# The opening of a two-layer hybrid trunk: another order of loads, plain products for half of the inner dimension, and a bank of its own for the first compression

## The chip, the cores and the metric

One core of one Trainium2 chip runs the whole program. The metric is the device time of one execution in microseconds. The kernel before took 2611.32 us (median of three runs, from 2610.13 to 2612.88).

## The reference

Two layers work on `x` of 1024 positions by 1024 features, with a condition `c` of 1024 numbers. Cut to what this case needs:

```python
cond = jax.nn.silu(c)
for l in range(2):
    mod = cond @ w_mod[l] + b_mod[l]                       # 6 x 1024
    sh1, sc1, gt1, sh2, sc2, gt2 = split(mod, 6)
    h = rms_norm(x, norm_g[l, 0]) * (1.0 + sc1) + sh1
    p = h @ w_in[l]                                        # 22 blocks of 128 columns
    outs = [conv(p), sparse_attention(p), linear_attention(p), gmlp(p)]
    y = rms_norm(outs, grp_gain[l]) @ w_o[l]
    x = x + gt1 * rms_norm(y, norm_g[l, 1])
    h = rms_norm(x, norm_g[l, 2]) * (1.0 + sc2) + sh2
    y = jnp.square(jax.nn.relu(h @ w_up[l])) @ w_down[l]
    x = x + gt2 * rms_norm(y, norm_g[l, 3])
```

The sparse attention compresses its keys and values first: windows of 32 positions of `k_cmp` and `v_cmp`, with the rows of `cmp_pos` added, go through `silu(z @ cmp_w1) @ cmp_w2`. Queries and keys of its other two branches (selected and sliding window) are rotated by cosine and sine of `positions`.

## The kernel before, in words

Activations lie with features on partitions: a tile is 128 features by T = 512 positions, and `x` is two halves of eight such tiles. A product of the projections is made in three products of a rounded type (`mm3`, L174 to L177): each operand is split into a rounded `hi` (a cast on ACT) and the rest `lo` (a subtraction on DVE), and TensorE adds `hi*hi`, `hi*lo` and `lo*hi`. Products of two plain fp32 operands are used where tiles are small, for the sums over partitions with a matrix of ones (L199) and for transposes.

`start()` (L269) is the opening of layer 0, first half:
- `rope_tables()` (L346 to L390) loads the frequencies, a selection matrix and the positions, makes cosine and sine in some 30 small DVE steps, spreads them with TensorE through a bank of tag `s`, and stores four tables to DRAM (L390).
- `cond` is loaded in two halves, spread over all partitions, and takes `silu` (L293 to L296).
- `load_x` loads eight tiles; `rms_R` (L190 to L199) squares them on ACT, adds the squares on DVE, and makes one product with `ones`; `rstd` (L202) gives R by two activations, `Ln` and `Exp`.
- for each of eight k: two rows of `w_mod` (shift and scale) are loaded (128 x 1024, L276) and each is multiplied by `cond` and summed on DVE (`mod_dot`, L239 to L243); `make_h` (L207 to L215) makes `h` of k as `hi` and `lo`; six column blocks of `w_in` (`EARLY`, 10 and 17 to 21) take their products of this k, each in a PSUM bank of its own (two of `mm`, two of `ff`, two of `s`). The weights of these blocks come in two halves of four k (`wload`, L279), and are split at k = 0 and k = 4 (`wsplit`, L284).
- `load_params` (L107) loads the small vectors of both layers on SP's queue.

Everything behind it is in `mix(0, 0, ...)`. There are lanes of streamed weights, each with its own buffers: `a` (always there), `b` (region "wb", opened at L925 for the first `mix` alone) and `f` (for the feed-forward part). A region takes its memory where an earlier region was closed; a tile in it waits for the last use of what lay there. `start()` has regions "kw" (right side), "su" and "rp". In the first `mix` the remaining sixteen column blocks go through `gemm` (L179) in lane `b`: two halves of four k, each one load (L158), one split (L167 and L131) and twelve products; beside each half, a step of `mods_now` (L322) loads and multiplies one more row of `w_mod` in two halves (`mod_half`, L245 to L251, loads into `raw_b`). The sparse attention (`nsa_part`) runs between them: `compress` (L702 to L756), then for each of four blocks of 128 positions scores (L829, L831), softmax, and `attend` (L780 to L790): four transposes of the weights into the one bank of tag `t`, a cast, a subtraction, two products into the bank of tag `pv`. I call one such group an attention unit. Each of the four mixers ends in a group norm (`group_out`, L218, with a product with `ones`), and then the eight gemms with `w_o` start (lane `a`).

PSUM has eight banks: two each of `mm`, `ff` and `s`, one of `t` and one of `pv` (L58). `compress` takes four tiles in turn from `mm`, the tag that the gemms use:

```python
            hx = partial(lambda jj, i: k5[:, jj, i // 8:i // 8 + 32, 2 * (i % 8)])
            hp_ = ps("mm", (128, 2, 32))
...
                hb = partial(lambda jj, i: pos2[:, jj, 2 * i:2 * i + 32])
                pb = ps("mm", (128, 2, 2))
```

`hx` is the pass over the keys and values (32 small products, L717), `hb` the same pass over the position rows, which are loaded at L732.

The order on each engine is not written by hand: the whole kernel stands in a block whose scheduler lists the instructions of each engine from a simulated time line, so an edit in one place moves instructions in others. One queue, SP's, issues all DMAs.

Of the kernel before, what the change touches and what calls it, by code (L numbers as in the profile page):

```python
# [35 lines left out]
def trunk_kernel(ctx, tc, xT, c, pos, freq, sel, w_in, conv_w, cmp_pos, cmp_w1, cmp_w2,  # L36
# [10 lines left out]
    def region(name, side="left"):  # L47
        return tc.tile_pool(name=name, bufs=1, reuse_waits="tile", side=side)
# [58 lines left out]
    def load_params(l, names):  # L107
        src = {"ng": norm_g, "bmod": b_mod, "conv": conv_w, "gain": gains}
        for n in names:
            dma(out=par[l][n], in_=src[n][l])  # L110
# [95 lines left out]

    def make_h(xt, R, Ac, shc, ks=range(8)):  # L207
        h = []
        for k in ks:
# [59 lines left out]
    def start():  # L269
        d = par[0]  # L270
        early = {}
        rope_tables()
        with region("kw", "right") as kw, region("su") as su:
            def mk(src, shape):
                t = su.tile(shape, F32, name="mw", tag="mw", bufs=4)
                dma(out=t, in_=src)  # L276
                return t

            def wload(n, kh):  # L279
                raw = kw.tile([128, 4, 128], F32, name="raw_k", tag="raw_k", bufs=6)  # L280
                dma(out=raw, in_=w_in[0, n, :, 4 * kh:4 * kh + 4, :])
                return raw

            def wsplit(raw):  # L284
                hi, lo = (kw.tile([128, 4, 128], F32R, name="w_k", tag="w_k", bufs=12) for _ in range(2))
                A.copy(hi, raw)
                sub(lo, raw, hi.bitcast(F32))
                return hi, lo

            for hf in range(2):  # L290
                t1, t2 = (su.tile([128, T], F32, name="ct", tag="ct", bufs=4) for _ in range(2))
                ch = cond[:, hf * T:hf * T + T]
                dma(out=ch, in_=c[:, hf * T:hf * T + T].to_broadcast([128, T]))  # L293
                logsig(t2, ch, t1)
                A.activation(t2, t2, AF.Exp)
                mul(ch, ch, t2)  # L296
            xt = load_x(0)
            load_params(0, ("ng", "bmod"))
            R = rms_R(xt, 1.0 / 1024)
            bm = d["bmod"].rearrange("p (j k) -> p j k", k=8)  # L300
            hs = []
            for k in range(8):
                ma = work.tile([128, 2, 1], F32, name="ma", tag="ma", bufs=4)
                for j in (0, 1):
                    mod_dot(0, j, k, mk, ma[:, j, :])
                add(d["mod"][:, 0:2, k:k + 1], ma, bm[:, 0:2, k:k + 1])
                mod_scale(0, 1, slice(k, k + 1))
                if k % 4 == 0:
                    raws = [wload(n, k // 4) for n in EARLY]
                hs += make_h(xt, R, d["A1"], d["mod"][:, 0, :], (k,))  # L310
                if k % 4 == 0:
                    ws = {n: wsplit(r) for n, r in zip(EARLY, raws)}
# [6 lines left out]
        load_params(1, ("ng", "bmod", "conv", "gain"))  # L319
        return hs, early  # L320

# [24 lines left out]
    def rope_tables():  # L346
        with region("rp") as rp:
# [3 lines left out]
            fr = rp.tile([128, 1, 8], F32, name="fr")  # L351
            dma(out=fr, in_=freq.unsqueeze(0).to_broadcast([128, 1, 8]))
            sl = rp.tile([17, 256], F32, name="sl")
            dma(out=sl, in_=sel)
            pi = rp.tile([128, 8, 1], I32, name="pi")
            dma(out=pi, in_=pos.unsqueeze(2))
# [22 lines left out]
            for hf in range(2):  # L379
# [5 lines left out]
                for w, dst in ((0, cosd), (128, sind)):  # L385
                    p = ps("s")
# [243 lines left out]
    def nsa_part(l, hf, h, rg, gates, early={}):  # L630
# [70 lines left out]

        def compress():  # L702
# [8 lines left out]
            def partial(col):  # L711

                hid = ps("mm", (128, 2, 128))
# [9 lines left out]
            hx = partial(lambda jj, i: k5[:, jj, i // 8:i // 8 + 32, 2 * (i % 8)])  # L723
            hp_ = ps("mm", (128, 2, 32))
            for jj in range(2):
                PE.matmul(hp_[:, jj, :], hx[:, jj, :], sel4, start=True, stop=True)
            if hf == 0:
# [7 lines left out]
                pb = ps("mm", (128, 2, 2))  # L735
                for jj in range(2):
                    PE.matmul(pb[:, jj, :], hb[:, jj, :], sel4[:, 0:2], start=True, stop=True)
                A.copy(posb[l], pb[:, :, 0:1])
            hs = pt((128, 2, 32))
# [5 lines left out]
            kc = ps("mm", (128, 2, 64))  # L745
# [6 lines left out]
            vc = ps("mm", (128, 64))  # L752
# [314 lines left out]

    h, early = start()
# [96 lines left out]
```

## Time and profile before

| | before |
|---|---|
| median of three runs | 2611.32 us |
| profiled execution | 2618.0 us |
| its span | 2616.3 us |
| PE (TensorE) busy | 2488.0 us, 95% |
| PEld (its weight loads, beside PE) | 1985.6 us, 76% |
| DVE (VectorE) busy | 1631.3 us, 62% |
| ACT (ScalarE) busy | 1308.9 us, 50% |
| POOL (GpSimd) busy | 53.9 us, 2% |
| DMA | 305.79 MB, mean 117 GB/s |
| chain that ended last | PE 83%, DVE 8%, DMA 5%, ACT 2%, issue 1% |

The profile shows one execution; its own time is 1.7 us above its span and 6.7 us above the median. Busy time is the time in which an engine worked on instructions; the chain is the work followed back from the last instruction, at each step to what released it. The granted clock is the share of TensorE's full clock that it had in a stretch. In the rows below a line number stands before each operation (L175), and "out<-in" are the program's names.

### The profile page before, as it was taken

The page shows a single profiled execution, that of the slowest core. Times are in us where ns is not written, and L with a number is a line of the kernel's source. Part 1 is how long each engine was busy: PE and PEld are TensorE (multiplying, and loading weights), DVE is VectorE, ACT ScalarE, POOL GpSimd, SP SyncE. Part 2 cuts the span into 40 slices and gives each one's busy share as a digit, 9 for nine tenths or more (in the row PEclk, how much of TensorE's full clock was granted, in tenths as well). Part 3 has the DMA queues.
Part 4 walks back from the last instruction along what each step waited for, and adds up shares of the span by engine and source line. Part 5 has one row for each costly group of instructions (what it writes and reads, how often), then busy time and mean ns, then how long its engine had stood idle before and what let it go on. Part 6 is the DMA issues. An engine that isn't in the chain of part 4 may idle for free.

```text
span 2616.3 us, 34392 instructions
## 1 busy us (share of the span) xinstructions
PE 2488.0 (95%) x11834; PEld 1985.6 (76%) x11834; DVE 1631.3 (62%) x3425; ACT 1308.9 (50%) x2657; POOL 53.9 (2%) x65
## 2 busy tenths in 40 slices
PE   5798899999999999999999999999999997999997
PEld 3666677777777878887787787877788875788886
DVE  7697675467887587445676476554577745634445
ACT  3465545445565456344365455444466744443433
POOL 0100000010000000000100000000100000000000
PEclk9898899999999999999999999999999999999999
DMA  8443233355434444223423354322422134333332
GB/s 280 141 151 94 91 122 121 110 152 153 127 117 142 153 157 146 93 78 105 146 77 92 94 157 141 103 81 77 121 74 69 61 107 150 127 98 97 97 97 75
DMA packets 176200, 305.79 MB, mean 117 GB/s; under 512 B 21573, under 2 KB 33434, under 8 KB 176026
## 3 DMA queue, kind: packets, MB, share of 16 engines
q1 hardware_dynamic: 176026, 303.60, 37.6%
q8 instruction: 93, 1.52, 0.2%
q14 instruction: 81, 0.66, 0.1%
HBM read 281.50 MB, written 17.83 MB: 114 GB/s over the span
## 4 chain that ended last, share of the span: by engine, by line
PE 83%; DVE 8%; DMA 5%; ACT 2%; issue 1%; SPq 0%; DVEq 0%; ACTq 0%
PE ps_ff L175 17%; PE ps_ff L176 17%; PE ps_ff L177 17%; PE ps_mm L176 7%; PE ps_mm L177 7%; PE ps_mm L175 7%; DMA raw_f<-in_w_mod_dram 2%; PE ps_mm L784 1%; DMA raw_b<-in_w_mod_dram 1%; PE ps_pv L790 1%; PE ps_pv L789 1%; PE ps_s L829 1%; PE ps_t L199 1%; PE ps_s L831 1%; PE ps_t L784 1%
## 5 line engine op out<-in xcount | busy, mean ns | idle before, releaser
L167 ACT CAST w_f<-raw_f 128x512 fp32r<-128x512 f32 x504 | 311.8, 619 | 430.5 <-PE ps_ff L176 409.0
L131 DVE TENSOR_TENSOR w_f<-raw_f,w_f 128x512 fp32r<-128x512 f32 x504 | 350.7, 697 | 177.7 <-ACT w_f L167 166.6
L175 PE MATMUL ps_ff<-hid,w_f 128*128 128x512 f32 x992 | 395.2, 399 | 21.4 <-DVE yf L137 12.7
L177 PE MATMUL ps_ff<-h,w_f 128*128 128x512 f32 x1024 | 405.4, 396 | 1.2 <-DVE w_f L131 1.2
L176 PE MATMUL ps_ff<-h,w_f 128*128 128x512 f32 x1024 | 402.7, 393 | 0.0
L175 PE MATMUL ps_ff<-h,w_f 128*128 128x512 f32 x1024 | 402.7, 393 | 0.0
L176 PE MATMUL ps_ff<-hid,w_f 128*128 128x512 f32 x992 | 392.1, 395 | 1.5 <-DVE hid L131 1.5
L177 PE MATMUL ps_ff<-hid,w_f 128*128 128x512 f32 x992 | 391.3, 394 | 0.0
L175 PE MATMUL ps_mm<-h,w_a 128*128 128x512 f32 x784 | 317.1, 405 | 6.2 <-ACT h L226 5.1
L177 PE MATMUL ps_mm<-h,w_a 128*128 128x512 f32 x784 | 315.7, 404 | 6.7 <-DVE w_a L131 6.7
L176 PE MATMUL ps_mm<-h,w_a 128*128 128x512 f32 x784 | 313.6, 401 | 1.2 <-DVE h L131 1.2
L167 ACT CAST w_a<-raw_a 128x512 fp32r<-128x512 f32 x196 | 121.3, 620 | 297.7 <-PE ps_mm L176 276.8
L131 DVE TENSOR_TENSOR w_a<-raw_a,w_a 128x512 fp32r<-128x512 f32 x196 | 135.0, 690 | 171.2 <-ACT w_a L167 167.3
L175 PEld LDWEIGHTS ps_ff<-hid,w_f 128*128 128x128 f32 x992 | 187.8, 189 | 69.7 <-DVE yf L137 15.2
L177 PEld LDWEIGHTS ps_ff<-h,w_f 128*128 128x128 f32 x1024 | 192.3, 188 | 45.8 <-issue 3.4
L175 PEld LDWEIGHTS ps_ff<-h,w_f 128*128 128x128 f32 x1024 | 192.4, 188 | 42.6 <-issue 3.1
L176 PEld LDWEIGHTS ps_ff<-h,w_f 128*128 128x128 f32 x1024 | 192.4, 188 | 42.0 <-issue 2.2
L176 PEld LDWEIGHTS ps_ff<-hid,w_f 128*128 128x128 f32 x992 | 187.9, 189 | 44.4 <-issue 2.9
L177 PEld LDWEIGHTS ps_ff<-hid,w_f 128*128 128x128 f32 x992 | 187.8, 189 | 41.2 <-issue 1.4
L137 DVE TENSOR_TENSOR y<-y,ps_ff 128x512 f32<-128x512 f32 (+1 forms) x208 | 138.0, 664 | 123.7 <-PE ps_ff L177 122.4
L175 PEld LDWEIGHTS ps_mm<-h,w_a 128*128 128x128 f32 x784 | 149.3, 190 | 45.8 <-ACT h L226 6.7
L177 PEld LDWEIGHTS ps_mm<-h,w_a 128*128 128x128 f32 x784 | 149.0, 190 | 44.9 <-DVE w_a L131 8.6
(390 smaller groups left out, 3618.3 us busy)
## 6 DMA issues: line engine op xcount, KB each, us to landing
raw_f<-in_w_up_dram SPq DMA_DIRECT2D x256, 256.0 KB, 2.7
raw_f<-in_w_down_dram SPq DMA_DIRECT2D x256, 256.0 KB, 2.7
raw_a<-in_w_in_dram SPq DMA_DIRECT2D x132, 256.0 KB, 2.7
raw_f<-in_w_mod_dram SPq DMA_DIRECT2D x112, 256.0 KB, 2.8
raw_a<-in_w_o_dram SPq DMA_DIRECT2D x64, 256.0 KB, 2.7
raw_b<-in_w_mod_dram SPq DMA_DIRECT2D x48, 256.0 KB, 2.9
mw<-in_w_mod_dram SPq DMA_DIRECT2D x16, 512.0 KB, 5.1
bp<-in_cmp_w_dram SPq DMA_DIRECT2D x32, 256.0 KB, 5.3
```

The costliest lines, as they stand in the source:

```text
L131: V.tensor_tensor(out=out, in0=a, in1=b, op=ALU.subtract)
L137: eng.tensor_tensor(out=out, in0=a, in1=b, op=ALU.add)
L167: A.copy(hi, raw)
L175: PE.matmul(ps_ap, wh, xh, start=start, stop=False)
L176: PE.matmul(ps_ap, wh, xl, start=False, stop=False)
L177: PE.matmul(ps_ap, wl, xh, start=False, stop=stop)
L199: PE.matmul(p, ones, acc, start=True, stop=True)
L784: PE.transpose(tp[0:kn, hh, :], cols(h0 + hh), ident)
L789: PE.matmul(pv[:, h0:h0 + nh, :], vst, th[0:kn], start=first[0], stop=False)
L790: PE.matmul(pv[:, h0:h0 + nh, :], vst, tl[0:kn], start=False, stop=last)
L829: PE.matmul(sp[:, 0:w], qh[:, h0 + hh, :], KX[:, 128 * k0:128 * k0 + w], start=True, stop=False)
L831: PE.matmul(sp[:, 0:w], ql[:, h0 + hh, :], KX[:, 128 * k0:128 * k0 + w], start=False, stop=True)
```

## The change

Five things are done.
1. `start()`: `cond` is loaded first (SP), then two rows of `w_mod`, then `x`, then the six `w_in` halves and the next four rows; the small vectors and the three inputs of the tables go to POOL's queue (`P.dma_start`). Two more buffers take rows of `w_mod` (6 instead of 4), and rows are loaded three k ahead. The second halves of the six blocks lie in buffers of tag `h`.
2. The squares of `x` are summed by TensorE: eight fp32 products with `ones`, one for each k, in place of seven additions on DVE and one product.
3. For the first four k the six blocks take one plain fp32 product each, of the raw weights and the unsplit `h`, in place of three products of split operands. `h` of each k is still split, since the later gemms use it. `x` is multiplied by R first, and one activation with scale and shift makes `h`. The six splits of the first halves go away; those of the second halves stand behind k = 1.
4. `rope_tables` comes last in the code of `start()`, and its products take the bank of `pv`.
5. Region "wb" is opened before `start()` (it no longer lies where the opening's buffers lay). In the first `mix` `compress` takes its four tiles from the bank of `pv`, and the pass over the position rows stands ahead of the pass over keys and values, in every `mix`.

```diff
+        with region("kw", "right") as kw, region("rp") as rp, region("su") as su:
...
+            for c_ in halves:
+                dma(out=cond[:, c_], in_=c[:, c_].to_broadcast([128, T]))
+            load_params(0, ("ng", "bmod"), P.dma_start)
+            small = rope_loads(rp)
+            mws = {0: mload(0)}
+            xt = load_x(0)
+            raws = [wload(n) for n in EARLY]
+            mws[1] = mload(1)
+            mws[2] = mload(2)
+            late = [wlate(n) for n in EARLY]
...
-            R = rms_R(xt, 1.0 / 1024)
+            p = ps("t")
+            for k in range(8):
+                sq = nt()
+                A.activation(sq, xt[k], AF.Square)
+                PE.matmul(p, ones, sq, start=k == 0, stop=k == 7)
+            R = rstd(p, 1.0 / 1024, su.tile([128, T], F32, name="R0"))
...
+                if k + 3 < 8:
+                    mws[k + 3] = mload(k + 3)
+                mul(xt[k], xt[k], R)
+                t = su.tile([128, T], F32, name="ct", tag="ct", bufs=4)
+                A.activation(t, xt[k], AF.Identity, scale=d["A1"][:, k:k + 1], bias=d["mod"][:, 0, k:k + 1])
+                hs.append(split(t))
                 for i, n in enumerate(EARLY):
...
-                    hi, lo = ws[n]
-                    mm3(early[n], hi[:, k % 4, :], lo[:, k % 4, :], hs[k][0], hs[k][1], k == 0, k == 7)
-        load_params(0, ("conv", "gain"))
+                    if k < 4:
+                        PE.matmul(early[n], raws[i][:, k, :], t, start=k == 0, stop=False)
+                    else:
+                        hi, lo = late[i]
+                        mm3(early[n], hi[:, k - 4, :], lo[:, k - 4, :], hs[k][0], hs[k][1], False, k == 7)
+                if k == 1:
+                    late = [wsplit(r) for r in late]
+            rope_tables(rp, *small)
+        load_params(0, ("conv", "gain"), P.dma_start)
...
-                    p = ps("s")
+                    p = ps("pv")
...
+        CT = "pv" if (l, hf) == (0, 0) else "mm"
...
-                hid = ps("mm", (128, 2, 128))
+                hid = ps(CT, (128, 2, 128))
...
-                with region("wb", "right") as lane_pool["b"]:
+                with wbs:
...
+    wbs = ExitStack()
+    lane_pool["b"] = wbs.enter_context(region("wb", "right"))
     h, early = start()
```

SP's queue, from the program's start, before (tables' inputs, `cond` and `x` first, then small vectors and weights; `mw` are the rows of `w_mod`):

```order
L352 DMA fr<-in_freq_dram 128x8
L354 DMA sl<-in_sel_dram 17x256
L356 DMA pi<-in_pos_dram 128x8
L293 DMA cond<-in_c_dram 128x512 x2
L1064 DMA y<-in_xT_dram 128x512 x8
L110 DMA ng_96<-in_norm_g_dram 128x32
L110 DMA bmod_97<-in_b_mod_dram 128x48
L281 DMA raw_k<-in_w_in_dram 128x512 x6
...
L281 DMA raw_k<-in_w_in_dram 128x512 x2
L390 DMA cosd<-of 128x512
L276 DMA mw<-in_w_mod_dram 128x1024 x2
```

and now (`raw_b` are the buffers of lane `b`):

```order
L299 DMA cond<-in_c_dram 128x512 x2
L275 DMA mw<-in_w_mod_dram 128x1024 x2
L1096 DMA y<-in_xT_dram 128x512 x8
L280 DMA raw_k<-in_w_in_dram 128x512 x6
L275 DMA mw<-in_w_mod_dram 128x1024 x4
L285 DMA w_r<-in_w_in_dram 128x512 x6
L275 DMA mw<-in_w_mod_dram 128x1024 x2
L158 DMA raw_a<-in_cmp_w_dram 128x128
L158 DMA raw_b<-in_w_in_dram 128x512
L158 DMA raw_b<-in_w_mod_dram 128x512 x2
```

The first rows of `w_mod` moved from behind `x`, the small loads and ten of the weight loads to the second place, and the first loads of lane `b` stand among the opening's.

PE right behind the last products of the opening, before (L717 is a pass of `compress`, `w2g` and `tri` belong to the linear attention, L829 and L831 are the scores of the first attention unit):

```order
L177 MATMUL ps_s<-h,w_k 128x512
L717 MATMUL ps_mm<-bp,kvt 32x128 x32
L507 MATMUL ps_ff<-w2g,lrT 128x128 x3
L486 MATMUL ps_t<-ident,nt 128x64 x4
L507 MATMUL ps_ff<-w2g,lrT 128x128
L690 MATMUL ps_t<-ident,p 128x128 x4
L512 MATMUL ps_ff<-tri,g 128x128 x4
L726 MATMUL ps_mm<-sel_124,p 128x32 x2
L717 MATMUL ps_mm<-bp,p 32x128 x32
L829 MATMUL ps_s<-KS,qh 128x128
```

and now:

```order
L177 MATMUL ps_s<-h,w_k 128x512
L516 MATMUL ps_t<-ident,nt 128x64 x4
L175 MATMUL ps_mm<-h,w_b 128x512
L176 MATMUL ps_mm<-h,w_b 128x512
L177 MATMUL ps_mm<-h,w_b 128x512
L175 MATMUL ps_mm<-h,w_b 128x512
```

The gemms of lane `b` stand directly behind the opening, and both passes of `compress` moved in between later gemms.

PE from the last product of lane `b` to the first with `w_o` (L175 with `w_a`), before:

```order
L177 MATMUL ps_mm<-h,w_b 128x512
L199 MATMUL ps_ff<-nt,ones 128x512
L199 MATMUL ps_t<-nt,ones 128x512
L175 MATMUL ps_mm<-h,w_a 128x512
```

and now (`bp` and `p` are softmax weights; L816, L821 and L822 are one attention unit; of its seven the first two and the last stand here):

```order
L177 MATMUL ps_mm<-h,w_b 128x512
L822 MATMUL ps_pv<-w_a,VS 128x512
L816 MATMUL ps_t<-ident,bp 128x128 x4
L821 MATMUL ps_pv<-w_a,VS 128x512
L822 MATMUL ps_pv<-w_a,VS 128x512
L816 MATMUL ps_t<-ident,bp 128x128 x4
L199 MATMUL ps_ff<-nt,ones 128x512
...
L816 MATMUL ps_t<-ident,p 32x128 x4
L821 MATMUL ps_pv<-w_a,VC 128x512
L822 MATMUL ps_pv<-w_a,VC 128x512
L199 MATMUL ps_t<-nt,ones 128x512
L175 MATMUL ps_mm<-h,w_a 128x512
```

Before, all attention units stood ahead of the last gemm of the lane, whose product is the first row; now seven stand behind it.

## Rows read from the trace of the kernel before

**Rows 1.** Windows; columns as in the first line, then window and its length.
```profile
core 0: us, PE busy (x) PEld busy (x) DVE busy (x) ACT busy (x) POOL busy (x), PEclk, DMA share, GB/s
0.00:75.50 75.50, 46.32 (x162) 31.79 (x162) 53.10 (x130) 28.20 (x49) 2.52 (x10) 1.00 0.80 274
75.50:107.80 32.30, 16.24 (x188) 14.00 (x187) 24.77 (x72) 12.86 (x43) 7.81 (x6) 0.66 0.41 118
107.80:160.00 52.20, 50.69 (x302) 40.54 (x301) 43.05 (x146) 33.01 (x89) 0.53 (x1) 0.98 0.53 159
160.00:288.60 128.60, 106.94 (x489) 76.61 (x488) 94.38 (x241) 67.03 (x153) 5.52 (x8) 0.92 0.35 107
288.60:400.00 111.40, 107.59 (x434) 84.96 (x435) 80.06 (x125) 58.35 (x97) 0.00 (x0) 0.94 0.37 118
400.00:2616.00 2216.00, 2160.20 (x10266) 1737.73 (x10264) 1335.95 (x2716) 1109.41 (x2229) 37.52 (x41) 0.99 0.36 111
```

**Rows 2.** Timeline of the first 41 us; [idle before <- releaser] at the end.
```profile
start us, us, engine line op out<-in xcount [idle before <-releaser]
...
4.13 0.17 DVE L358 CAST pf<-pi 128x8 f32<-128x8 int32 x1 [1.24 <-DMA pi<-in_pos_dram]
...
8.43 0.19 DVE L377 TENSOR_SCALAR sc<-n 128x64 f32<-128x64 f32 x1
...
22.80 1.19 SPq L276 DMA_DIRECT2D mw<-in_w_mod_dram  x2
...
26.77 2.05 PE L199 MATMUL ps_t<-nt,ones 128*128 128x512 f32 x2 [5.62 <-DVE nt L137]
...
29.96 0.62 ACT L204 ACTIVATE nt<-nt 128x512 f32<-128x512 f32 x1
...
30.82 1.22 DVE L243 CUSTOM_DVE_ANT_0 mw<-mw,cond 128x1024 f32<-128x1024 f32 x1
...
40.75 1.22 PE L175 MATMUL ps_mm<-h,w_k 128*128 128x512 f32 x2 [11.93 <-ACT h L213]
```

**Rows 3.** Lines of 40 to 76 us by form: the weight splits of the opening.
```profile
line engine op names shapes xcount | busy us, mean ns | idle before us <-releasers
...
L131 DVE TENSOR_TENSOR w_k<-raw_k,w_k 128x512 fp32r<-128x512 f32 x6 | 3.9, 685 | 0.0
...
L286 ACT CAST w_k<-raw_k 128x512 fp32r<-128x512 f32 x6 | 3.3, 616 | 2.0 <-PE ps_mm L176 2.0
```

**Rows 4.** Chain of waits: start, length, what; two rounded products, one fp32 product.
```profile
47.26 0.45 PE ps_mm L175 x2
...
245.18 0.86 PE ps_ff L199 x2
```

**Rows 5.** Windows, 20 to 40 us, columns as in rows 1.
```profile
20.00:40.00 20.00, 3.20 (x4) 0.50 (x2) 15.12 (x29) 9.08 (x18) 0.00 (x0) 1.00 0.94 330
```

**Rows 6.** DMA issues of the first 60 us; KB each, median us to landing.
```profile
bmod<-in_b_mod_dram SPq DMA_DIRECT2D x2, 24.0 KB, 4.0
```

**Rows 7.** Chain of waits from 75 to 130 us.
```profile
92.47 0.58 SPq L732
...
95.28 3.64 PE ps_mm L717 x64
...
120.00 0.68 DVE w_b L131
```

**Rows 8.** Timeline behind the opening, columns as in rows 2.
```profile
74.49 0.35 SPq L158 DMA_DIRECT2D raw_b<-in_w_in_dram  x1
...
109.81 0.69 DVE L131 TENSOR_TENSOR w_a<-ps_t,w_a 128x512 fp32r<-128x512 f32 x1
...
221.90 0.60 PE L784 MATMUL ps_t<-ident,bp 128*128 128x128 f32 x4
...
224.77 1.06 PE L784 MATMUL ps_t<-ident,bp 128*128 128x128 f32 x4
...
253.12 0.67 DVE L131 TENSOR_TENSOR w_a<-ps_t,w_a 32x512 fp32r<-32x512 f32 x1
...
275.16 0.39 PE L177 MATMUL ps_mm<-h,w_b 128*128 128x512 f32 x1
...
288.61 0.79 PE L175 MATMUL ps_mm<-h,w_a 128*128 128x512 f32 x1 [5.09 <-ACT h L226]
```

More of the change, by code (lines that the diff above doesn't have):

```diff
@@ L105, in trunk_kernel, with load_params @@
         par.append(d)
-    def load_params(l, names):
+    def load_params(l, names, load=dma):
         src = {"ng": norm_g, "bmod": b_mod, "conv": conv_w, "gain": gains}
         for n in names:
-            dma(out=par[l][n], in_=src[n][l])
+            load(out=par[l][n], in_=src[n][l])
     KS = const.tile([128, 1024], F32R, name="KS")
@@ L205, in rstd, with make_h @@
         return R
-    def make_h(xt, R, Ac, shc, ks=range(8)):
+    def make_h(xt, R, Ac, shc):
         h = []
-        for k in ks:
+        for k in range(8):
             t = nt()
@@ L288, in wsplit, with mload @@
                 return hi, lo
-            for hf in range(2):
+            def mload(k):
+                return [mk(w_mod[0, 8 * j + k], [128, 1024]) for j in (0, 1)]
+            halves = [slice(hf * T, hf * T + T) for hf in range(2)]
+            for c_ in halves:
[8 more added lines that the diff above has]
+            late = [wlate(n) for n in EARLY]
+            for c_ in halves:
                 t1, t2 = (su.tile([128, T], F32, name="ct", tag="ct", bufs=4) for _ in range(2))
-                ch = cond[:, hf * T:hf * T + T]
-                dma(out=ch, in_=c[:, hf * T:hf * T + T].to_broadcast([128, T]))
-                logsig(t2, ch, t1)
+                logsig(t2, cond[:, c_], t1)
                 A.activation(t2, t2, AF.Exp)
-                mul(ch, ch, t2)
-            xt = load_x(0)
-            load_params(0, ("ng", "bmod"))
-            R = rms_R(xt, 1.0 / 1024)
+                mul(cond[:, c_], cond[:, c_], t2)
+            p = ps("t")
+            for k in range(8):
+                sq = nt()
+                A.activation(sq, xt[k], AF.Square)
+                PE.matmul(p, ones, sq, start=k == 0, stop=k == 7)
+            R = rstd(p, 1.0 / 1024, su.tile([128, T], F32, name="R0"))
             bm = d["bmod"].rearrange("p (j k) -> p j k", k=8)
@@ L303, in start @@
                 ma = work.tile([128, 2, 1], F32, name="ma", tag="ma", bufs=4)
-                for j in (0, 1):
-                    mod_dot(0, j, k, mk, ma[:, j, :])
+                for j, raw in enumerate(mws.pop(k)):
+                    V.tensor_tensor_reduce(out=raw, in0=raw, in1=cond, scale=1.0, scalar=0.0,
+                                           op0=ALU.mult, op1=ALU.add, accum_out=ma[:, j, :])
                 add(d["mod"][:, 0:2, k:k + 1], ma, bm[:, 0:2, k:k + 1])
                 mod_scale(0, 1, slice(k, k + 1))
[L308 to L312, printed above, removed]
+                if k + 3 < 8:
[4 more added lines that the diff above has]
+                hs.append(split(t))
                 for i, n in enumerate(EARLY):
@@ L721, in partial @@
                 return hs
[L723 to L726, printed above, removed]
             if hf == 0:
@@ L738, in compress @@
                 A.copy(posb[l], pb[:, :, 0:1])
+            hx = partial(lambda jj, i: k5[:, jj, i // 8:i // 8 + 32, 2 * (i % 8)])
+            hp_ = ps(CT, (128, 2, 32))
+            for jj in range(2):
+                PE.matmul(hp_[:, jj, :], hx[:, jj, :], sel4, start=True, stop=True)
             hs = pt((128, 2, 32))
@@ L744, in compress @@
             mul(hs, hs, act)
-            kc = ps("mm", (128, 2, 64))
+            kc = ps(CT, (128, 2, 64))
             for r in range(2):
```

38 lines of the change are left out of this document (21 added, 17 removed).

## The prediction

> **What bounds the kernel now.** I read the busy time by stretches first. From 288.6 us on (the first product with `w_o`) PE is busy 107.6 of 111.4 us and then 2160.2 of 2216.0 us [rows 1]: nothing that ends earlier on another engine shortens that part, and what starts earlier moves all of it. Before 288.6 us PE is busy 46.3 of 75.5, 16.2 of 32.3, 50.7 of 52.2 and 106.9 of 128.6 us; DVE is busy 215.3 of the 288.6 us. So the part that can be won lies ahead of 288.6 us, and it is idle time of two engines that take turns.
>
> The timeline of the opening comes next. The first product of the input projection starts at 40.75 us, after 11.93 us in which PE waited for ACT's `h` [rows 2]. `h` waits for the modulation: the first `w_mod` dot runs at 30.82 us, because `cond` is ready only then and because SP issues the `w_mod` loads from 22.80 us on, behind `x`, `raw_k` and the small loads. From 40.75 us PE is dense: 144 products at 0.225 us (two rounded ones take 0.45 [rows 4]) end at 75.8 us.
>
> Then the chain of waits: the stretch from 75.5 to 107.8 us is the compression. The position rows are issued at 92.47 us, its second pass ends at 98.9 us, and the first weights of the `b` lane, whose buffers lie where the opening's lay, are loaded only from 74.5 us on; the third gemm of that lane begins its weight split at 120.00 us [rows 7, 8]. PE's granted clock there is 0.66 of full on average [rows 1], between its two levels of 1.2 and 2.4 GHz, after PE had been busy only half the time.
>
> **The opening, step by step.** Bytes first. The DMA engines carry 330 GB/s when nearly full [rows 5], and move little before 2.5 us. SP's new order puts 0.5 MB of `cond`, 1.05 MB of `w_mod` and 2.1 MB of `x` ahead of the rest: `x` is in at 3.67/0.33 + 2.5 = 13.6 us. `cond` (in at about 5 us) takes two chains of ACT and DVE steps of 0.6 to 0.7 us, some 7 us: ready at 11.7 us. The dots of the first `k`, 2 x 1.22 us [rows 2], end at 14.1; the tables' small DVE steps, which stand there in DVE's order and took 4.5 us from 4.13 us on [rows 2], end near 18.6.
>
> The sum of squares is now eight fp32 products instead of one. One, recorded as two instructions, costs 2.05 us where PE comes from 5.62 us of idling [rows 2] and 0.86 us in a dense stretch [rows 4]. Three at the first price and five at the second, from the first square at 10.2 us (5 + 8 x 0.62, behind the chains' steps on ACT), end near 20; `Ln` and `Exp` (0.62 each, [rows 2]) make `R` at 21; one multiply and one activation later the first product starts at about 22.7 us, 18 us before now.
>
> PE's work: 24 plain products at 0.86 us replace 72 at 0.225, that is 20.6 for 16.2 us, and seven more products with `ones` cost 6.0 us. All 10.4 us lie in time in which PE waits anyway. DVE loses seven adds (4.8 us) and six weight splits of 0.685 us (4.1 us), ACT six casts of 0.616 us (3.7 us) [rows 3]. The second half of the weights is cast while `w_mod` is awaited; if that cover went, the six casts (3.7 us) would stand ahead of the fifth `k`.
>
> The pace is set by `w_mod`: up to its last pair SP's order has 16 loads of 512 KB, 38 of 256 KB (six already for the `b` lane, four of the second half's `x`, four stores of the tables) and one of 64 KB, 18.4 MB: 18.4/0.33 + 2.5 = 58 us. Dots, scale, activation, cast and split behind it take 4.6 us, the last 18 products 4.1: the opening ends at **66.7 us**, 9 us before now. At 274 GB/s, the mean of the first 75 us [rows 1], it would be 70 us and 78; without any limit by bytes PE alone needs 22.7 + 36.8 = 59.5.
>
> **From there to the third gemm of the `b` lane.** The lane's buffers are there from the start, so its first two half-gemms are loaded and split in the opening. DVE's order puts, between the last pair's dots and the third gemm's first split: 2 dots (2.4 us), 18 full-width steps (half dots, splits, adds, shuffles, copies) at about 0.69 us [rows 3] and small ones (2.7 us), 17.5 us. Two waits come in: the `kvt` copies wait for the last products (4 us) and the rotary adds for POOL (2 us). 58 + 23.5 = **82 us against 120.00**: 38 us. The compression no longer holds this up: it has its own bank and PE runs it between the gemms, position rows first.
>
> **From there to `w_o`.** From 120.00 us to the last gemm of the lane at 275.6 us [rows 8] pass 155.5 us in which PE is busy 87% and DVE 76% of the time [rows 1]. The same gemms, dots and attention units come in another mixture, so I keep the 155.5 us: last gemm at 237.5. What comes behind it is longer. Now all units of the attention are done by then, and 13.4 us of group norms lead to `w_o` at 288.61. In the changed order seven units stand behind the last gemm: four transposes into the only bank of `t`, ACT's cast, DVE's subtraction, two products, and the next may not begin earlier. From one unit's transposes to the next's took 2.87 us in such a place [rows 8]: 20 us. Then two copies, two adds and one group norm, 8 to 9 us as now. 28.5 us instead of 13.4 gives 15 of the 38 us back: `w_o` starts at 266, **23 us earlier**. Bounds: units at 2.2 us (their three steps alone) give 28 us, at 6.2 us (143.3 us for 23 steps now, [rows 8]) give none.
>
> Behind `w_o` the order of every engine is that of before, so the 23 us arrive at the end. The edits to `make_h`, `load_params`, the order inside `compress` and its bank have no other cost there. The profiled execution takes 2618.0 us, its span is 2616.3, 6.7 us over the median of the runs: 2618.0 - 23 = 2595 there, **2588** for the median.
>
> **The small loads on POOL's queue.** The trace has no DMA of that queue. On SP's a 24 KB load took 4.0 us to land [rows 6]; `b_mod` is first needed at 14 us, and a delay to 21 us is hidden by `R`. So I take nothing; bounds 0 and the rival below. The Trainium skill, SBUF — State Buffer, section Who interferes with whom, says that descriptors of DMAs issued from GpSimd are written by that engine, which DVE's two-port modes lock out, and advises the SP or ACT queue; no run here shows it yet. By that rule the loads come late by DVE's copies, which are few here.
>
> **The rivals.**
> - *More comes through* (22%). The units left for the end take some 6 us of PE out of the 155.5 us, and of PE's idle time there (21.7 of the last 128.6 us [rows 1]) as much again goes; with units of 2.2 us the gain is about 38: 2573 us. For it: that idle time is made of waits for other steps, which a new mixture can fill. Against: PE is idle only 1.5 of the first 52.2 us.
> - *The middle stretches* (14%). The lane runs ahead of the attention, DVE's dots push the attention's steps back, and 155 us become 170: gain 8, 2603 us.
> - *The end eats it* (5%). The seven units keep the 6.2 us they have now: 43 us instead of 20, gain 0, 2611 us.
> - *Slower: the attention's chain starts late* (5%). It has 24 units, from 109.81 to 253.12 us now [rows 8], with 22 us to spare before the last gemm. In the new order the spare time is gone and `w_o` starts 157 us after the first unit's subtraction (143.3, the last products, and the norm). I put that at 108 us (DVE has 26 us of work between the third gemm's split and it), which again gives 265. It waits for keys, for the position rows and for eight `qh`, `ql` copies on SP's queue, behind loads that wait for the last `k` and for the opening's buffers. Each us costs one; from 137 us on the kernel is over 5 us slower. At 145: 2625 us.
> - *POOL's loads are late* (2%). If `b_mod` landed 20 us late, the first half of the opening would slip by 13 us, of which the bytes hide half: 2595 us.
>
> **How the numbers follow.** The forecast with gains from 12 to 34 us has 52%. About 0.2%, 5 us, can be told from no change. Faster: 52 + 22 + 2 and most of the 14, 86%. Slower 5%, the rest 9%. The range takes in both rates of the DMA, units of 2.2 to 4 us, the stronger case and the stretched middle: 2568 to 2606.
>
> **What would show it.** First plain product near 23 us; last `w_mod` dot near 59; end of the opening near 67; no hole of 32 us behind it; third gemm's first split near 82; last gemm near 237; seven units alone behind it at 2 to 3 us each at the lower clock level; `w_o` near 266; the same time as now from there to the end. It is wrong if the opening ends later than 75 us, if the first attention unit comes after 125 us, or if the part behind `w_o` changes.

## The result, and the profile after

The changed kernel takes 2594.48 us (median of four runs, 2589.17 to 2597.75) against 2612.10 us for the kernel before in the same comparison (four runs, 2610.13 to 2615.17). The ratio is 0.992, with a 95% interval from 0.9904 to 0.9935: 17.6 us less, and the interval is clear of 1. Forecast were 23 us, a median of 2588 and a range from 2568 to 2606; the time lies in it. In a second comparison, on the chip of the last experiments (e12), the changed kernel stood at 0.9907 (0.9890 to 0.9924), 24.6 us under the kernel before. A gain of 20 to 25 us lies in both intervals.

| | before | after |
|---|---|---|
| span of the profiled execution | 2616.3 us | 2591.4 us |
| PE busy | 2488.0 us | 2493.2 us |
| DVE busy | 1631.3 us | 1620.7 us |
| ACT busy | 1308.9 us | 1313.1 us |
| first product of the opening | 40.75 us | 23.46 us |
| third gemm of lane `b`, first split | 120.00 us | 82.43 us |
| first product with `w_o` | 288.61 us | 275.95 us |
| from there to the end of the span | 2327.7 us | 2315.4 us |

The two spans differ by 24.9 us, the medians by 17.6, since the profiled execution of before lies some 6 us above its median. Within the spans, 12.7 us were won ahead of `w_o` and 12.2 us behind it. The forecast had 23 ahead and none behind.

The milestones of the changed kernel, as its timeline has them (start, length, engine, line, operation; [rows 2] and [rows 8] hold those of before): the first plain product, the last product of the opening, the third gemm's first split, the subtraction of the first attention unit, the last product of lane `b`, the subtraction of the last unit, and the first product with `w_o`.

```profile
23.46 1.88 PE L338 MATMUL ps_mm<-ct,raw_k 128*128 128x512 f32 x4
...
68.29 0.39 PE L177 MATMUL ps_s<-h,w_k 128*128 128x512 f32 x1
...
82.43 0.68 DVE L131 TENSOR_TENSOR w_b<-raw_b,w_b 128x512 fp32r<-128x512 f32 x1
...
116.78 0.69 DVE L131 TENSOR_TENSOR w_a<-ps_t,w_a 128x512 fp32r<-128x512 f32 x1
...
245.22 0.40 PE L177 MATMUL ps_mm<-h,w_b 128*128 128x512 f32 x1
...
264.37 0.68 DVE L131 TENSOR_TENSOR w_a<-ps_t,w_a 32x512 fp32r<-32x512 f32 x1 [2.34 <-ACT w_a L818]
...
275.95 0.80 PE L175 MATMUL ps_mm<-h,w_a 128*128 128x512 f32 x1 [3.85 <-ACT h L226]
```

Windows over the same stages, of before (columns as in rows 1): the opening; from its end to `w_o`; in that, from the third gemm to the last product of lane `b`, and what stands behind that product.

```profile
0.00:75.40 75.40, 46.22 (x161) 31.79 (x162) 53.00 (x130) 28.10 (x49) 2.42 (x10) 1.00 0.80 274
75.40:288.60 213.20, 173.97 (x976) 131.15 (x974) 162.31 (x457) 112.99 (x284) 13.96 (x15) 0.89 0.40 122
...
120.00:275.20 155.20, 141.92 (x731) 106.22 (x729) 120.36 (x341) 83.49 (x200) 5.41 (x8) 0.96 0.38 118
275.20:288.60 13.40, 3.52 (x6) 0.80 (x4) 8.47 (x13) 9.40 (x18) 0.63 (x1) 0.69 0.54 178
```

And of the changed kernel:

```profile
0.00:68.30 68.30, 55.00 (x152) 29.20 (x152) 48.63 (x133) 31.83 (x53) 7.93 (x20) 0.95 0.90 329
68.30:276.00 207.70, 177.98 (x977) 128.94 (x975) 157.23 (x443) 111.25 (x281) 14.85 (x15) 0.91 0.38 116
245.20:276.00 30.80, 16.92 (x50) 8.28 (x48) 15.89 (x26) 15.70 (x28) 0.64 (x1) 0.64 0.27 89
...
82.40:245.20 162.80, 146.96 (x857) 109.30 (x856) 128.17 (x393) 86.86 (x233) 7.50 (x9) 0.95 0.39 118
```

The second line of each fence is the one to read first. The opening ends 7.1 us earlier, and the whole stretch from there to `w_o` is only 5.5 us shorter (207.7 for 213.2 us), although the third gemm begins 38 us earlier in it. PE has the same 976 or 977 recorded products in both and idles 39 us before, 30 us after. By the other lines, 16 us of the idle time of before lay between the opening and the third gemm, and none lies there now; ahead of the lane's last product it has grown by 2.6 us and behind it by 4.0. The same number of products also keeps PE busy 4.0 us longer (178.0 for 174.0 us); behind the last product its granted clock is 0.64.

Behind `w_o` most of the gain lies at one place, the compression of layer 1, first half. SP issues the eight loads of its weights (`cmp_w`, into `bp`) 15.8 us earlier than before, and the end of the span comes 24.9 us earlier. The first line is before, the second after:

```profile
1270.77 3.78 SPq L708 DMA_DIRECT2D bp<-in_cmp_w_dram  x8
```

```profile
1254.97 5.55 SPq L740 DMA_DIRECT2D bp<-in_cmp_w_dram  x8
```

PE's timeline there, before:

```profile
1274.96 1.04 PE L717 MATMUL ps_mm<-bp,kvt 128*32 128x128 f32 x16 [1.05 <-DMA bp<-in_cmp_w_dram]
...
1281.59 0.66 PE L717 MATMUL ps_mm<-bp,kvt 128*32 128x128 f32 x8 [0.72 <-DMA bp<-in_cmp_w_dram]
1282.18 0.80 PE L176 MATMUL ps_ff<-hid,w_f 128*128 128x512 f32 x1
```

and as windows:

```profile
1270.00:1281.60 11.60, 7.53 (x72) 4.13 (x72) 5.69 (x13) 0.60 (x1) 3.80 (x3) 0.81 0.78 253
1281.60:1287.60 6.00, 6.00 (x21) 4.51 (x22) 2.82 (x7) 1.61 (x3) 0.00 (x0) 0.52 0.12 23
```

PE's timeline after:

```profile
1264.98 0.39 PE L177 MATMUL ps_ff<-h,w_f 128*128 128x512 f32 x1
1267.10 1.96 PE L749 MATMUL ps_mm<-bp,p 128*32 128x128 f32 x64 [1.73 <-DMA p<-in_cmp_pos_dram]
```

and a window:

```profile
1257.00:1267.10 10.10, 8.37 (x38) 6.62 (x38) 7.95 (x17) 3.09 (x5) 2.55 (x2) 1.00 0.80 263
```

Before, the pass over the keys came first, at the moment when its weights `bp` were being loaded: PE takes it piece by piece from 1274.96 to 1282.2 us as they land, and products of the feed-forward part that have all they need stand behind it. Then PE runs 6 us with a granted clock of 0.52, about its lower level of 1.2 GHz. After, the pass over the position rows stands first, and since those are loaded behind `bp`, the scheduler lists it later: feed-forward products fill the time of the loads, PE waits 1.73 us, and the clock stays at 1.00.

### The profile page after: what moved, and what is told of

Its sections match the earlier page's. It is cut to its first block, busy times and chain, and to the rows that moved or that the text cites. A ratio compares the mean times of both kernels' runs of the same rounds, so it can differ in the third digit from the quotient of the medians.

```text
span 2591.4 us, 34346 instructions
## 1 busy us (share of the span) xinstructions
PE 2493.2 (96%) x11824; PEld 1976.8 (76%) x11824; DVE 1620.7 (63%) x3412; ACT 1313.1 (51%) x2659; POOL 60.6 (2%) x76
## 4 chain that ended last, share of the span: by engine, by line
PE 85%; DVE 7%; DMA 5%; issue 1%; ACT 1%; SPq 0%; DVEq 0%; ACTq 0%
PE ps_ff L175 17%; PE ps_ff L176 17%; PE ps_ff L177 17%; PE ps_mm L175 7%; PE ps_mm L176 7%; PE ps_mm L177 7%; DMA raw_f<-in_w_mod_dram 3%; DMA raw_b<-in_w_mod_dram 1%; PE ps_pv L822 1%; PE ps_pv L821 1%; PE ps_mm L816 1%; PE ps_s L861 1%; PE ps_t L199 1%; PE ps_t L816 1%; PE ps_s L863 1%
## 5 line engine op out<-in xcount | busy, mean ns | idle before, releaser
L175 PE MATMUL ps_ff<-hid,w_f 128*128 128x512 f32 x992 | 393.3, 397 | 18.0 <-DVE yf L137 12.7
L175 PE MATMUL ps_ff<-h,w_f 128*128 128x512 f32 x1024 | 402.4, 393 | 2.7 <-ACT nt L192 2.7
L175 PE MATMUL ps_mm<-h,w_a 128*128 128x512 f32 x784 | 317.2, 405 | 4.7 <-ACT h L226 3.9
L175 PEld LDWEIGHTS ps_ff<-hid,w_f 128*128 128x128 f32 x992 | 187.0, 188 | 65.5 <-DVE yf L137 15.2
L175 PEld LDWEIGHTS ps_ff<-h,w_f 128*128 128x128 f32 x1024 | 192.4, 188 | 45.8 <-issue 3.1
L177 PEld LDWEIGHTS ps_ff<-hid,w_f 128*128 128x128 f32 x992 | 186.9, 188 | 40.8 <-issue 1.1
L175 PEld LDWEIGHTS ps_mm<-h,w_a 128*128 128x128 f32 x784 | 149.3, 190 | 44.5 <-ACT h L226 5.4
```

Of the source, the lines that this page charges most:

```text
L175: PE.matmul(ps_ap, wh, xh, start=start, stop=False)
L177: PE.matmul(ps_ap, wl, xh, start=False, stop=stop)
```

## The experiments

The theories after the result: (A) the order of the two passes saves some 9 us in layer 1; (C) ahead of `w_o` the stretch behind the opening keeps its length whatever is moved in it, so that only an earlier end of the opening counts. Rivals: the gain in layer 1 was an accident of one profile; lane `b` alone, or the attention's chain alone, sets `w_o`. Milestones of all runs, in us from their timelines ("middle" is from the last product of the opening to `w_o`, the ratio is against the kernel before on the same chip):

| run | first product | end of opening | third gemm | first, last unit | last of lane b | w_o | middle | ratio (95%) |
|---|---|---|---|---|---|---|---|---|
| before | 40.8 | 75.4 | 120.0 | 109.8, 253.1 | 275.2 | 288.6 | 213.2 | 1 |
| after | 23.5 | 68.3 | 82.4 | 116.8, 264.4 | 245.2 | 276.0 | 207.7 | 0.992 (0.9904 to 0.9935) |
| e1 | 41.5 | 76.9 | 121.8 | 111.6, 253.5 | 275.5 | 288.9 | 212.0 | 0.9972 (0.9963 to 0.9982) |
| e2 | 24.3 | 69.2 | 83.4 | 116.7, 263.0 | 243.8 | 274.6 | 205.4 | 0.993 (0.9917 to 0.9944) |
| e3 | 23.3 | 67.8 | 115.3 | 98.5, 240.9 | 263.6 | 277.5 | 209.7 | 0.9928 (0.9914 to 0.9942) |
| e4 | 23.8 | 68.5 | 85.0 | 110.1, 258.9 | 251.1 | 272.6 | 204.1 | 0.99 (0.9887 to 0.9914) |
| e5 | 24.8 | 69.7 | 85.5 | 114.6, 263.1 | 255.4 | 276.9 | 207.2 | 0.9908 (0.9893 to 0.9924) |
| e6 | 23.7 | 68.5 | 163.2 | 95.1, 151.9 | 298.1 | 311.6 | 243.1 | 1.0062 (1.0045 to 1.0079) |
| e7 | 25.0 | 70.6 | 86.8 | 117.6, 264.7 | 257.0 | 278.4 | 207.8 | 0.9927 (0.9913 to 0.9942) |
| e8 | 26.1 | 70.0 | 86.6 | 117.2, 262.7 | 255.0 | 276.5 | 206.5 | 0.9909 (0.9894 to 0.9924) |
| e9 | 40.7 | 75.1 | 109.2 | 117.2, 274.3 | 269.3 | 289.3 | 213.9 | 0.997 (0.9954 to 0.9987) |
| e10 | 24.0 | 68.9 | 83.0 | 103.0, 163.8 | 310.3 | 324.7 | 255.8 | 1.0105 (1.009 to 1.012) |
| e11 | 23.6 | 68.2 | 84.9 | 107.6, 164.4 | 315.4 | 329.1 | 260.9 | 1.0106 (1.0089 to 1.0123) |
| e12 (after, again) | 23.8 | 68.6 | 82.8 | 117.6, 262.8 | 243.6 | 274.3 | 205.7 | 0.9907 (0.989 to 0.9924) |

### The order of the two passes in layer 1 (e1, e2)

e1 is the kernel before with the position rows first in layer 1 alone, e2 the changed kernel with the keys first there:

```diff
-            hx = partial(lambda jj, i: k5[:, jj, i // 8:i // 8 + 32, 2 * (i % 8)])
...
+            if l == 1:
+                hx = partial(lambda jj, i: k5[:, jj, i // 8:i // 8 + 32, 2 * (i % 8)])
```

> The kernel before, with one edit: in layer 1 alone the pass of compress over the position rows stands ahead of the pass over keys and values. Theory A (the order of the two passes saves a wait in layer 1): the stall of PE near 1275 us, where the pass over the keys waits for the loads of cmp_w1, goes, w_o of layer 0 stays at 288.6 us, and the kernel is 8.7 us faster than before, 2603 us. Rival (those 8.7 us were an accident of the profiled run, the whole gain comes from the opening): no change, 2611 to 2612 us.

> The changed kernel, with the old order of the two passes in layer 1 alone. Theory A: w_o of layer 0 still near 276 us, the stall of layer 1 is back, 8.7 us slower than the changed kernel: 2603 us, 9 below before. Rival (accident): 2594.5 us, 17.6 below before.

e1 won 0.28%, 7.3 us of 2617.8, with an interval from 4.7 to 9.7 us. e2 lost 3 or 6 us against the changed kernel (0.993 for 0.992 or, in e12, 0.9907); those intervals overlap, so its time alone settles nothing. `w_o` is where it was in both kernels (288.9, 274.6). The stall is gone in e1, where PE waits 0.92 us ahead of the position rows, and back in e2 (timelines):

```profile
1284.01 1.96 PE L717 MATMUL ps_mm<-bp,p 128*32 128x128 f32 x64 [0.92 <-DMA p<-in_cmp_pos_dram]
```

```profile
1256.10 0.46 PE L749 MATMUL ps_mm<-bp,kvt 128*32 128x128 f32 x8 [1.58 <-DMA bp<-in_cmp_w_dram]
...
1259.52 2.83 PE L749 MATMUL ps_mm<-bp,kvt 128*32 128x128 f32 x32 [0.21 <-DMA bp<-in_cmp_w_dram]
```

Theory A holds, by e1's time and the stall in both profiles: one edit of order, far from the opening, makes about 7 us. The profiles of all runs agree. From SP's first load of `cmp_w` in layer 1 to the end of the span it takes 1345.5 us before and 1343.7 in e2, the two with the keys first, and 1336.1 to 1340.2 us in the twelve others. Between `w_o` and that load there is a smaller difference, 982.2 and 983.7 us before and in e1 against 975.4 to 980.4 in the others; it was not followed up.

### The bank of the first compression (e3, e9)

e3 is the changed kernel with `CT = "mm"`; e9 is the kernel before with nothing but the changes to `compress` (bank and order):

```diff
-        CT = "pv" if (l, hf) == (0, 0) else "mm"
+        CT = "mm"
```

> The changed kernel, with compress of the first mix in the tag mm again. Theory A (the bank of its own is what lets the gemms pass the compression): both passes stand right behind the opening, the third gemm of lane b begins its split at 95 to 105 us instead of 82.4, but the attention starts some 10 us earlier and no unit is left behind the last gemm; w_o near 276 to 283, time 0 to 7 us above the changed kernel. Rival (the attention's chain alone sets w_o, and it gains what the gemms lose): w_o near 268, 2587 us.

> The kernel before, with the changes to compress alone: the bank of pv in the first mix, and the position rows first in every mix; opening, loads and lane b's region as before. Theory C (from the end of the opening to w_o it takes 204 to 210 us whatever the order inside, so the stretch of 32 us that the bank frees comes back later): opening ends at 75 to 77, third gemm 10 us or more earlier than 120, w_o at 280 to 287; with the 6 us of layer 1 the time is 8 to 14 us under before. Rival D (the bank is worth the 32 us of the compression, and only the new opening spoilt it): w_o at 265 or earlier.

In e3 the third gemm begins at 115.3 us, later than expected: with the compression in `mm` the gemms are held 33 us, so the bank does let them pass it. Yet `w_o` starts only 1.5 us later, since the attention begins 18 us earlier and nothing is left behind the last gemm but the norms (13.9 us). e9 says the same from the other side, and more strongly than expected: the third gemm comes 10.8 us earlier than before, `w_o` not at all (289.3 for 288.6 us). Its gain of 0.3% is that of e1. The middle as windows, e3 and e9:

```profile
67.80:277.50 209.70, 174.51 (x977) 130.82 (x976) 158.43 (x442) 110.43 (x282) 14.24 (x15) 0.89 0.37 115
```

```profile
75.40:289.30 213.90, 173.42 (x975) 128.84 (x974) 162.35 (x459) 111.71 (x283) 13.14 (x15) 0.91 0.39 121
```

Theory C holds in these two, but for the sizes of e9: `w_o` had been expected at 280 to 287 us and a gain of 8 to 14 us, and 6.9 us came. By itself the bank does not bring `w_o` forward; it exchanges the order of lane and attention.

e9 and e12 (the changed kernel again) were compared with the same runs of the kernel before. Between them lie the new opening and lane `b`'s early region: `w_o` at 289.3 and 274.3 us, medians of 2609.83 and 2592.13 us. So the greater part of the gain, some 15 to 18 us, comes with the opening.

### Lane b's region and its buffers (e4, e5)

e4 opens the region in the first `mix`, as before; e5 gives the lane four raw buffers:

```diff
-                with wbs:
+                with region("wb", "right") as lane_pool["b"]:
```

```diff
-    RAWB = {"a": 3, "f": 5, "b": 3}
+    RAWB = {"a": 3, "f": 5, "b": 4}
```

> The changed kernel, with region wb opened in the first mix again, so that its buffers lie where the opening's lay. Theory A (lane b sets w_o): its first splits wait for the end of the opening at 66.5 us, the third gemm begins at 92 to 97 instead of 82.4, and w_o starts 8 to 14 us later, 2603 to 2608 us. Rival (the attention's chain sets w_o): first unit still near 117 us, w_o within 4 us of 276, 2591 to 2598 us.

> The changed kernel, with four instead of three raw buffers in lane b (and, to find the memory, 15 instead of 16 buffers of the small softmax statistics). Theory B (the lane's own loop, load, split, dots, next load in three buffers, sets its pace and with it w_o): the ten splits from the third gemm on, 53.4 us in the changed kernel, take 45, the last gemm ends 8 us earlier and w_o starts at 267 to 271. Rival A (the attention's chain through the single bank of t sets w_o): the lane runs further ahead, w_o stays within 3 us of 276.

In e4 the first split of the lane comes 19 us later (55.3 for 36.1 us, now still inside the opening), the third gemm 2.6 us later, and `w_o` 3.4 us earlier; the time is that of e12 within the interval. So the early region buys nothing that can be measured; what brings the third gemm from 120 to 82 is the bank together with the shorter opening. e5 did nothing either: DVE still waits 9.2 us for the rows of `w_mod` in its ten splits (10.5 us in the changed kernel's 54 us), they take 57.0 us instead of 53.4, and `w_o` stays. So theory B fell: a fourth buffer does not quicken the lane. The waits of the two:

```profile
DVE raw_b L251 <- DMA raw_b<-in_w_mod_dram: 10.5, 10, 2.6
```

```profile
DVE raw_b L251 <- DMA raw_b<-in_w_mod_dram: 9.2, 12, 1.7
```

The first is the changed kernel from 82 to 136 us, the second e5 from 85.5 to 142.5 (us in total, times, longest).

### More banks for the attention's transposes (e6, e10, e11)

```diff
-            TG = ("t",) if (l, hf) == (0, 0) else TT
+            TG = TT
```

e10 has `("t", "ff")` in that place, and e11 that and the region of e4.

> The changed kernel, with the transposes of the first mix's attention in three banks (mm, mm, t) in turn, as in the later mixes. Theory A (the attention's chain through one bank sets w_o): the 24 units take under 135 us instead of 147.6, no serial units of 3 us stand behind the last gemm, w_o starts at 262 to 268, 8 to 13 us less time. Rival B (the lane and the sum of the work set it): what the attention gains the gemms lose, since both then take mm in turn, w_o within 4 us of 276.

> The changed kernel, with the transposes of the first mix's attention in two banks, t and one of ff in turn, so that the gemms keep both banks of mm. Theory E (the single bank of t makes the attention long, and the gemms were only starved where it took mm): third gemm at 82 to 95, no unit behind the last gemm, w_o at 262 to 270, 6 to 14 us less. Rival C (the sum of the stretch stays): w_o at 273 to 280, within 4 us of the changed kernel.

> As the run with t and ff, and region wb opened in the first mix as before, since that alone started w_o 3.4 us earlier. Theory E: w_o at 260 to 268. Rival C: w_o at 270 to 277.

All three are slower than the kernel before, by 0.6 to 1.1%, and both theories put forward for them fell. Theory C falls with them as far as it said whatever is moved: the middle grew to 243 to 261 us. The attention does get quick: its 24 units take 57 us in e6 and 61 in e10, instead of 148, and the seven units at the end are gone. But then the gemms have nothing beside them. In e10 a window from the end of the attention to the last product, and DVE's waits in it:

```profile
164.00:310.30 146.30, 118.58 (x544) 87.48 (x544) 82.40 (x201) 48.80 (x97) 4.78 (x8) 0.84 0.34 106
```

```profile
DVE raw_b L251 <- DMA raw_b<-in_w_mod_dram: 27.0, 17, 3.5
DVE w_b L131 <- ACT w_b L167: 17.9, 9, 5.3
```

From the third gemm to the last split the lane needs 130.5 us in e6, alone, for 27 steps of half a gemm: 4.8 us each, for twelve products that take 2.7 us at 0.225. In e10's window PE waits for the steps of the lane, and its clock is granted at 0.84 on average. In the changed kernel these 27 steps take 157.2 us, but the attention is done in their gaps. The single bank of `t`, which I took for a brake, seems to keep the two in step. That is not shown: the scheduler lists every engine's instructions anew for each of these edits, and no run gave the transposes more banks in an unchanged order.

### The opening's own edits (e7, e8)

e7 takes three rounded products for the first four k too, with their six splits; e8 adds the squares on DVE, with one product:

```diff
-                    if k < 4:
-                        PE.matmul(early[n], raws[i][:, k, :], t, start=k == 0, stop=False)
+                    hi, lo = raws[i] if k < 4 else late[i]
+                    mm3(early[n], hi[:, k % 4, :], lo[:, k % 4, :], hs[k][0], hs[k][1], k == 0, k == 7)
```

```diff
-            for k in range(8):
-                sq = nt()
-                A.activation(sq, xt[k], AF.Square)
-                PE.matmul(p, ones, sq, start=k == 0, stop=k == 7)
+            R = rms_R(xt, 1.0 / 1024)
```

> The changed kernel, with three rounded products of split operands for the first four k too, in place of one plain fp32 product. Theory P (from 32 us on the opening is bound by PE, 24 x 0.86 = 20.6 us against 72 x 0.225 = 16.2): the last product of the opening is issued 3 to 5 us earlier, near 64 instead of 68.3. Rival Q (the six more splits on ACT and DVE come first, or the bytes of w_mod set the end, as the prediction had it): first product 2 to 5 us later, last product at 67 to 71.

> The changed kernel, with the squares of x added on DVE and one product with ones, as before. The prediction had the seven more products in time in which PE waits anyway. Theory R (R waits for the row of eight products, 9.4 us of PE): R is ready 2 to 4 us earlier, the first plain product at 20 to 21.5 instead of 23.5, the opening ends 2 to 3 us earlier. Rival S (the adds stand behind cond and the first dots on DVE): first product at 24 to 28, opening's last product up to 3 us later.

Both theories fell. Rival S held, and rival Q in the end of the opening, but not in its first product, which had been expected 2 to 5 us later. Rounded products give PE less to do and yet end the opening 2.3 us later (first product 1.5 us later). They wait for split operands, and PE, idle for 4.0 us of the 45.6 from the first product to the last, works at a granted clock of 0.86 (the window, and the longest of PE's waits from 24 to 72 us):

```profile
25.00:70.60 45.60, 41.56 (x149) 30.66 (x148) 37.18 (x88) 19.53 (x33) 0.89 (x1) 0.86 0.89 324
```

```profile
PE ps_mm L175 <- ACT h L226: 3.4, 1, 3.4
```

The adds on DVE make the first product 2.6 us late and the end 1.7; from that product on PE has no idle time at all. In both, `w_o` follows by 0.5 to 2.5 us. The window of e8:

```profile
26.10:70.00 43.90, 43.90 (x134) 24.72 (x134) 34.23 (x86) 17.98 (x30) 0.00 (x0) 1.00 0.86 310
```

In e8 PE waits for the sum of squares until DVE has come to it:

```profile
PE ps_t L199 <- DVE nt L137: 20.0, 1, 20.0
```

These are small sizes against the 17 us by which the first product moved; the rest is put down to the rest of the new opening, the order of the loads and of `cond` above all, but that was not undone by itself and so is not shown.

### The changed kernel again (e12)

> The changed kernel itself, to compare on one chip with the runs sent along: 0.990 to 0.994 of before, w_o at 275 to 277.

It came out so, but for `w_o` at 274.3 us, 0.7 under what was expected: a milestone in this stretch moves by some 2 us from one execution to the next. No version beat the changed kernel by more than the intervals: e4, e5 and e8 stand at 0.990 to 0.991 like e12.

## Why the prediction was right, and where it was not

**The start of the opening: right.** First product at 23.46 us, forecast 22.7. The row of eight products with `ones` ran from 10.46 to 19.87 us (forecast 10.2 to 20), and e8 confirms that DVE would have been later.

**The end of the opening: near in size, wrong in cause.** The last product starts at 68.3 us and ends at 68.7; forecast was 66.7. I had the bytes of `w_mod` set the pace, at 330 GB/s. A window of the changed kernel shows more than that:

```profile
20.00:40.00 20.00, 17.29 (x36) 6.75 (x37) 18.57 (x40) 13.12 (x23) 0.00 (x0) 0.83 1.04 398
```

DVE is busy 18.6 of these 20 us and PE 17.3; the last dot starts at 55.09 us, earlier than the 58 us at which I had its data land. So the 330 GB/s of [rows 5] were no limit. From the first product on it is PE that holds the opening. It waits 1.3 us in all, twice for a bank in which the tables are spread, and from 40 us on not at all (windows, and PE's waits from 23 to 70 us):

```profile
23.46:30.00 6.54, 6.37 (x16) 2.38 (x14) 6.54 (x11) 1.12 (x4) 0.00 (x0) 1.00 1.04 393
30.00:40.00 10.00, 8.83 (x12) 3.33 (x13) 9.86 (x27) 8.79 (x16) 0.00 (x0) 0.66 1.03 400
40.00:68.30 28.30, 28.30 (x101) 18.65 (x99) 18.95 (x47) 7.82 (x14) 0.00 (x0) 1.00 0.81 291
```

```profile
PE ps_pv L417 <- ACT of L419: 1.3, 2, 0.7
```

The prediction gave PE 36.8 us for its 24 plain and 72 rounded products, if nothing else held them up; the stretch took 44.8. Two terms are missing in that sum. Three products that spread the tables (L417) stand between the first and the second k, and with their waits they take 5.7 us, from 28.6 to 34.3. And with a granted clock of 0.66 from 30 to 40 us the next four plain products take 5.8 us, where the first four took 3.4:

```profile
28.70 1.12 PE L417 MATMUL ps_pv<-nt,sl 17*128 17x512 f32 x2
30.50 1.12 PE L417 MATMUL ps_pv<-nt,sl 17*128 17x512 f32 x2 [0.67 <-ACT of L419]
32.30 2.07 PE L417 MATMUL ps_pv<-nt,sl 17*128 17x512 f32 x2 [0.68 <-ACT of L419]
34.30 3.78 PE L338 MATMUL ps_mm<-ct,raw_k 128*128 128x512 f32 x4
37.87 2.43 PE L338 MATMUL ps_ff<-ct,raw_k 128*128 128x512 f32 x4
40.14 1.88 PE L338 MATMUL ps_s<-ct,raw_k 128*128 128x512 f32 x4
```

So the plain products did not lie, as I wrote, in time in which PE waits anyway; they pay all the same, 2.3 us at the end of the opening, since without them the split operands come late (e7). Nor do 144 rounded products at 0.225 us lead from 40.75 to 75.8 us in the kernel before: that would be 32.4 us, and they took 35.

**The third gemm: right.** 82.43 us, forecast 82. The reason I gave first, buffers that are there from the start, is worth 2.6 us (e4); the second, the compression's own bank, is the one that counts (e3).

**From there to `w_o`: the step that failed.** "The same gemms, dots and attention units come in another mixture, so I keep the 155.5 us" was mis-sized by 7.6 us: the stretch took 162.8 us, and the last product of the lane came at 245.2 instead of 237.5 us. It was not the same work. The windows show 857 recorded products instead of 731, 5.0 us more of PE: both passes of `compress` and the first scores, which stood ahead of the third gemm before, now stand behind it. And PE idles 15.8 us in it instead of 13.3. The 87% for PE and 76% for DVE that I gave for these 155.5 us are those of 107.8 to 288.6 us; from 120.0 to 275.2 us it was 91% and 78%, so there was less idle time to fill than I had read. The tail was sized well: 30.8 us from the last product to `w_o`, forecast 28.5; its serial units come every 2.4 to 3.05 us, 2.9 on the mean, forecast 2.87, with PE's clock at 0.64. So `w_o` started at 276.0 instead of 266: 12.7 us won, not 23. I counted from a point inside the stretch; from the end of the opening the sum would have been seen at once, 213 us of shared PE, DVE and ACT time that e1 to e5 and e7 to e9 did not bring under 204 or over 214. Where the 4 to 9 us between old and new opening come from was not settled. e4 rules out the early region, but not work that moved into the opening. With the new opening the lane's first split runs inside it (at 36.1 us, 55.3 in e4, 81.9 before), and with the one bank of `t` DVE is then busy for 155 to 160 us of the middle, where it is for 162.3 in the three runs with the old opening. Whether that makes the difference was not tested.

**Behind `w_o`: missed.** "Behind `w_o` the order of every engine is that of before" was wrong, and the edit to `compress` was put at no cost. It moves the first pass of layer 1 behind some 30 feed-forward products, and that is the second part of the gain, about 7 us (e1). A change behind `w_o` was one of the signs by which the prediction called itself wrong. The two errors have opposite signs, 10 us too many ahead of `w_o` and none counted behind it. That the forecast of 23 us stands so near to the measured 17.6 and 24.6 is in part luck.

**The rivals.** *The middle stretches* came true by half: 162.8 us, where it had 170 for the 155 of the forecast. *The end eats it* did not occur, since the units at the end take 2.9 us and not 6.2. *Attention's chain starts late* was nearest in its sum: its first unit came at 116.8 us, 9 us behind the point that I gave, and `w_o` 159 us behind that, where the rival said 157. But in e3 the first unit comes 18 us earlier, and `w_o` does not: it is neither chain alone. *More comes through* did not occur, and e6 and e10 show why a quicker attention doesn't bring it. *POOL's loads are late* did not matter. They are in the DMA issues of the first 12 us:

```profile
bmod<-in_b_mod_dram POOLq DMA_DIRECT2D x2, 24.0 KB, 5.6
```

5.6 us from issue to landing, against 4.0 us on SP [rows 6], and the add that needs it ran at 14.10 us without a wait. That is no sign against the rule of the Trainium skill (SBUF — State Buffer, Who interferes with whom) that such loads can be held up by DVE; DVE ran no copy or cast ahead of 14.18 us, so these loads did not put it to the test.

## What to carry to other kernels

Where two chains share the engines, find the stretch in which they run together and take its length as a whole, from the event ahead of it to the event behind it; a stall removed in its middle can come back at its end (here 6.6 of 16 us of idle time came back, and slower products took 4.0 more). A resource that seems to throttle one chain may be what keeps the other supplied with gaps to fill, so price the widened resource with both chains in view. And compare the order of instructions over the whole program, not only around the edit: a pass that waits for its weights while runnable products stand behind it on the same engine is cheap to move, and here it was worth its wait and the lower clock behind it, about 7 us.

## What the runs showed of the hardware that was not expected

DMA moved 398 GB/s for 20 us while PE, DVE and ACT were busy, where the trace of before suggested 330. In layer 1 a pass that trickled along its loads for some 7 us (PE's granted clock 0.81 in that window) was followed by 6 us at 0.52. From PE's timeline, the 64 products of that pass took 8.3 us where they take 2.0 in one piece, and the next twelve took 5.2 us where twelve take 2.7 at 0.227: an estimate of 6 us lost in the stall and 2.5 us behind it.
